# Issuing the four stores of the rotary tables from GpSimd instead of ScalarE in a hybrid mixer and MoE layer

## The chip, the cores and the metric

One Trainium2 chip, one core. The metric is device time in microseconds (us) of one execution of the whole layer. TensorE is called PE in the profile, VectorE DVE, ScalarE ACT, GpSimd POOL, SyncE SP.

## What is computed

One layer of a conditioned decoder on 1024 tokens of width 1024: a modulated layer norm, one input projection `h @ w_in`, three branches that read it (a gated short convolution, a diagonal state space model called S5, and latent attention with rotary positions), their gated merge, and a mixture-of-experts feed-forward. The change touches the rotary tables and lies in time next to S5:

```python
inv_freq = ROPE_THETA ** (-jnp.arange(0, QK_ROPE, 2, dtype=jnp.float32) / QK_ROPE)
ang = positions.astype(jnp.float32)[..., None] * inv_freq
return jnp.cos(ang), jnp.sin(ang)
...
mag = jnp.exp(ar * dt)
lb_re = mag * jnp.cos(ai * dt)
lb_im = mag * jnp.sin(ai * dt)
...
_, _, s_re, s_im = lax.associative_scan(combine, (la_re, la_im, bu_re, bu_im), axis=1)
```

## The kernel before, in words

The order of every engine's instructions is set when the program is built. In the stretch `front` the orders of DVE, ACT and PE are written out by hand; elsewhere a scheduler places each instruction by times that it simulates, and it may slip instructions of other parts into the hand-written stretch. Each engine then works strictly in that order and waits where an operand is missing.

`front` normalises x, transposes it in eight column blocks j (PE, tile `ps_x`, L570), scales and shifts each block (ACT, `ht`, L579, then its rounded half `hh`, L583; DVE makes the rest `hl`, L587) and at once multiplies it with three column tiles of `w_in`, the S5 inputs u (PE, L596).

`s5_params` works on POOL alone: exponentials and one sine and cosine (`sincos`) of 144 columns, 16 for the S5 poles and 128 for the rotary angles. The results are `sn`, `cs` and the negated sine `nsn`. Four transfers (L791) write them to the DRAM tensor `csd`; it is read back much later, by L882 for the keys and by L1171 for the attention. From the first 16 columns POOL goes on to the pole powers `lam`, `bbar` and `z8`.

`s5_prep` runs for the four quarters q of S5. POOL computes the matrices `X` (L752 to L757 with 128x512 operands), the phase table `T` (the same lines, doubling from 4 columns) and clears a buffer `Y` (L990). PE transposes `X` (L968), ACT copies the result to `W` (L970), a small kernel matrix `kq` goes through eight ACT transfers into `Y` (L992), and DVE reorders it into `M` (L993). `s5_run` multiplies u by `W` (PE, L1013), rotates by `T`, scans and rotates back on DVE (L1021 to L1029, then L752 to L757 into `s`), and multiplies by `M` and `G` (PE, L1041 and L1046); ACT copies the sums (L1051) and SP stores them.

Between these PE steps the scheduler sets independent work of PE: the fourth u tile and the attention gates (`proj`, three matmuls L140 to L142 per block, with the weight tile split into `whi` by ACT, L125, and `wlo` by DVE, L129), then the projections for the attention in `proj_qkv` (L893, then tiles `cq`). DVE also has products for the convolution there (L342, L348) and, after S5, the norms of `proj_qkv` (L921 to L930).

Of the kernel before, what the change touches and what calls it, by code (L numbers as in the profile page):

```python
# [80 lines left out]
class K:  # L81
# [677 lines left out]
    def s5_params(self):  # L759

        nc, a, P = self.nc, self.a, self.s5p
        v = nc.gpsimd
        f = lambda n, *s: P.tile([128, *s], F32, name=n)
# [24 lines left out]
        csd = self.csd = self.dram.tile([2, 32, S], F32, name="csd")  # L788
        for dst, src in ((csd[0, 0:16], cs[:, 16:]), (csd[0, 16:32], cs[:, 16:]), (csd[1, 0:16], nsn[:]),
                         (csd[1, 16:32], sn[:, 16:])):  # L790
            nc.scalar.dma_start(out=dst.rearrange("f (b t) -> (f b) t", b=8), in_=src)  # L791

        self.lam = L = f("lam", 2, 9, 16)
        tmp = t_("ltmp", 4, 16)
# [17 lines left out]
        for i in range(9):  # L812
            src, dst = max(0, i - 3), max(0, i - 2)
# [1243 lines left out]
```

## Time and profile before

| quantity | us |
|---|---|
| time, median of 3 runs (1546.9 to 1547.45) | 1546.98 |
| the profiled execution, its own time | 1544.51 |
| its span, first to last instruction | 1542.8 |
| PE busy | 1391.5 |
| DVE busy | 950.7 |
| ACT busy | 478.9 |
| POOL busy | 373.7 |

The span is cut into views of windows, waits and timelines below; their times count from the start of the span, so 1.7 us of the profiled execution lie around it. The stretch that matters is 50 to 302 us.

### The profile page before, as it was taken

What the parts mean: (1) busy time and instruction counts of PE and PEld (TensorE: products, weight loads), DVE (VectorE), ACT (ScalarE), POOL (GpSimd) and SP (SyncE); (2) the same over time, 40 slices, a digit from 0 to 9 for tenths busy, and PEclk for the clock granted to TensorE, in tenths of its full rate; (3) what the DMA queues carried; (4) which work ended last, traced back from release to release, by engine and by line L of the source; (5) the groups of instructions that cost most, each with busy time, mean ns of one, the idle gap of its engine ahead of it and who ended that gap; (6) DMA issues with size and microseconds to landing.
All of it is one profiled execution on the core that took longest, in us unless ns stands there. A gap on an engine that the chain in (4) does not pass through costs nothing.

```text
span 1542.8 us, 19462 instructions
## 1 busy us (share of the span) xinstructions
PE 1391.5 (90%) x6866; PEld 990.3 (64%) x6866; DVE 950.7 (62%) x1652; ACT 478.9 (31%) x851; POOL 373.7 (24%) x571
## 2 busy tenths in 40 slices
PE   5589799479999999999799997999988999999966
PEld 3467678368888887787588886778887333333312
DVE  7464677899685555767477787868887111122128
ACT  6232112242223334222277774343611111111113
POOL 7999930000000000003501142510032111111110
PEclk9899999799999999999889999999999999999988
DMA  9232221132222237986500005654645798878726
GB/s 376 95 119 85 74 57 37 41 112 66 82 82 110 109 132 253 346 268 170 114 1 15 15 15 164 229 178 166 245 150 204 269 339 339 300 263 306 241 110 248
DMA packets 78056, 251.63 MB, mean 163 GB/s; under 512 B 15945, under 2 KB 27265, under 8 KB 68738
## 3 DMA queue, kind: packets, MB, share of 16 engines
q1 hardware_dynamic: 54096, 203.61, 38.4%
q10 hardware_dynamic: 15506, 25.73, 4.8%
q0 software_dynamic: 8352, 20.98, 4.2%
q8 instruction: 57, 0.93, 0.3%
q14 instruction: 45, 0.37, 0.1%
HBM read 302.53 MB, written 50.38 MB: 229 GB/s over the span
## 4 chain that ended last, share of the span: by engine, by line
PE 48%; issue 14%; DVE 13%; DMA 11%; POOL 10%; ACT 3%; ACTq 1%; SPq 0%; POOLq 0%; DVEq 0%
PE ps_mm L140 9%; PE ps_mm L141 9%; PE ps_mm L142 9%; DMA yd<-y,idx 7%; PE ps_up L140 3%; PE ps_up L141 3%; PE ps_up L142 3%; PE ps_O L1272 2%; PE ps_T L1258 2%; PE ps_S L140 1%; PE ps_S L142 1%; PE ps_S L141 1%; PE ps_y L1728 1%; POOL xg L1602 1%; POOL yd L1661 1%
## 5 line engine op out<-in xcount | busy, mean ns | idle before, releaser
L140 PE MATMUL ps_mm<-hh,wlo 128*128 128x512 f32 x304 | 123.4, 406 | 23.1 <-ACT sg L1075 15.5
L1138 POOL TENSOR_TENSOR mg<-mg,sg 128x512 f32<-128x512 f32 x16 | 23.4, 1474 | 496.0 <-DVE sg L1137 492.4
L1631 PE MATMUL ps_h<-wo,xt 128*64 128x512 f32 x480 | 130.9, 596 | 0.0
L142 PE MATMUL ps_mm<-hh,whi 128*128 128x512 f32 x304 | 122.8, 404 | 0.0
L141 PE MATMUL ps_mm<-hl,whi 128*128 128x512 f32 x304 | 122.4, 403 | 0.0
L1624 ACT COPY xt<-ps_tr 128x512 f32<-128x512 f32 x48 | 28.1, 585 | 245.9 <-PE ps_tr L1622 245.9
L1684 DVE TENSOR_TENSOR hd<-ps_h,hd 128x256 f32<-128x256 f32 x24 | 10.2, 425 | 126.9 <-ACT hd L1683 126.9
L1631 PE MATMUL ps_y<-wo,ht 128*64 128x512 f32 x288 | 87.6, 598 | 0.0
L125 ACT CAST whi<-raw 128x1024 fp32r<-128x1024 f32 (+1 forms) x45 | 46.8, 1040 | 129.9 <-PE ps_up L142 59.0
L1631 PE MATMUL ps_h<-ql,xt 128*64 128x512 f32 x192 | 87.0, 596 | 0.0
L140 PEld LDWEIGHTS ps_mm<-hh,wlo 128*128 128x128 f32 x304 | 58.7, 193 | 38.1 <-ACT sg L1075 16.1
L129 DVE TENSOR_TENSOR wlo<-raw,whi 128x1024 fp32r<-128x1024 f32 x44 | 61.1, 1388 | 26.6 <-ACT whi L125 26.6
L1631 PEld LDWEIGHTS ps_h<-wo,xt 128*64 128x64 f32 x480 | 38.6, 137 | 49.6 <-issue 49.6
L142 PEld LDWEIGHTS ps_mm<-hh,whi 128*128 128x128 f32 x304 | 58.6, 193 | 15.0 <-issue 1.1
L141 PEld LDWEIGHTS ps_mm<-hl,whi 128*128 128x128 f32 x304 | 58.8, 193 | 13.6 <-issue 0.2
L1602 POOL DMA_INDIRECT xg<-h2d,idx x26 | 26.4, 1015 | 166.5 <-PE ps_tr L1622 164.4
L1659 DVE SCALAR_TENSOR_TENSOR y<-ps_y,roww,g 128x512 f32<-128x512 f32 x48 | 36.0, 751 | 38.8 <-PE ps_y L1631 38.8
L1244 DVE TENSOR_REDUCE sm<-ps_S 128x1 f32<-128x256 f32 (+3 forms) x64 | 49.2, 770 | 10.7 <-PE ps_S L1241 10.3
L140 PE MATMUL ps_up<-ah,wlo 128*128 128x512 f32 x128 | 50.6, 403 | 5.2 <-ACT ah L125 2.9
L129 DVE TENSOR_TENSOR pl<-ps_T,ph 128x512 fp32r<-128x512 f32 (+1 forms) x80 | 45.9, 580 | 13.8 <-ACT ph L125 12.5
L140 PE MATMUL ps_mm<-wo,ml 128*128 128x512 f32 x128 | 50.0, 398 | 2.8 <-DVE sg L1354 2.8
L1648 DVE COPY ht<-ps_th 128x256 f32<-128x256 f32 x24 | 10.2, 424 | 67.5 <-PE ps_th L1646 67.5
(674 smaller groups left out, 3938.8 us busy)
## 6 DMA issues: line engine op xcount, KB each, us to landing
wo<-exp SPq DMA_DIRECT2D x110, 1024.0 KB
qh<-exp SPq DMA_DIRECT2D x26, 1024.0 KB
ql<-exp SPq DMA_DIRECT2D x26, 1024.0 KB
raw<-w_in SPq DMA_DIRECT2D x43, 512.0 KB
adr<-w_ada SPq DMA_DIRECT2D x32, 512.0 KB
wada<-w_ada SPq DMA_DIRECT2D x16, 512.0 KB
fy<-yd SPq DMA_DIRECT2D x16, 512.0 KB
sga<-sg ACTq DMA_DIRECT2D x8, 512.0 KB
```

What stands on the lines that cost most here:

```text
L125: nc.scalar.copy(out=hi, in_=src)
L129: e.tensor_tensor(out=lo, in0=src, in1=hi.bitcast(F32), op=ALU.subtract)
L140: mm(ps, wl, xh, start=first, stop=False)
L141: mm(ps, wh, xl, start=False, stop=False)
L142: mm(ps, wh, xh, start=False, stop=last)
L1244: v.tensor_reduce(out=sm[:], in_=x, axis=AX.XY if two else AX.X, op=ALU.max, negate=True)
L1258: pe.transpose(pt[:, k2 * 256 + qi * 128:k2 * 256 + qi * 128 + 128], prob[h, c, qi][:, ks], self.ident[:])
L1272: pe.matmul(po[:, 0:256], vv[:, kt, h].rearrange("p z d -> p (z d)"), x[z], start=kt == 0 and z == 0, stop=kt == 2 * c + 1 and z == 1)
L1602: self.nc.gpsimd.indirect_dma_start(out=self.xg[b % 2][:], out_offset=None, in_=self.h2d[:], in_offset=bass.IndirectOffsetOnAxis(ap=self.i ...
L1624: self.nc.scalar.copy(out=self.ex[b][:, n * 512:(n + 1) * 512], in_=ps[:])
L1631: self.nc.tensor.matmul(ps[z * 64:(z + 1) * 64, :], x[:, z * 64:(z + 1) * 64], w[z], start=first, stop=last, tile_position=(0, 64 * z))
L1659: nc.vector.scalar_tensor_tensor(out=y[:, sl], in0=ps[:], scalar=self.roww[:, b:b + 1], in1=self.g2[:, sl], op0=ALU.mult, op1=ALU.mult)
```

## The change

The loop that issues the four transfers calls GpSimd's queue instead of ScalarE's. Data, sizes and destinations stay the same.

```diff
         for dst, src in ((csd[0, 0:16], cs[:, 16:]), (csd[0, 16:32], cs[:, 16:]), (csd[1, 0:16], nsn[:]),
                          (csd[1, 16:32], sn[:, 16:])):
-            nc.scalar.dma_start(out=dst.rearrange("f (b t) -> (f b) t", b=8), in_=src)
+            nc.gpsimd.dma_start(out=dst.rearrange("f (b t) -> (f b) t", b=8), in_=src)
```

On ACT the four transfers stood between the pieces of `front`: two ahead of the two `ht` of block 6 and two behind them; they are gone there. On POOL they now stand in the middle of `s5_params`, at the end of `sincos`:

```order
 L787 TENSOR_SCALAR nsn<-sn 128x128
+L791 DMA csd<-sn 128x128
 L798 TENSOR_TENSOR lam<-mag,sn 128x16
 L811 COPY z_757<-sn 128x16
 L748 TENSOR_TENSOR cs_662<-c,p 128x144
+L791 DMA csd<-nsn 128x128
 L753 TENSOR_TENSOR ltmp<-lam 128x16
 L827 TENSOR_TENSOR t_626<-lam,par 128x16
 L829 TENSOR_TENSOR f_806<-lam,par 128x16
 L816 TENSOR_TENSOR z_757<-z_757 128x16
+L791 DMA csd<-cs_662 128x128 x2
```

Everything else of POOL moved only by a few places among its own rows.

Because the scheduler simulates other times, the other engines' orders shift. On PE, 60 gate and projection matmuls of 512 columns stand ahead of the first L968 instead of 44; the difference is 15 to 28 through most of S5 and closes by its end: 368 stand ahead of the last quarter's L1046 in both.

On DVE, in the third quarter's `s5_run` (`w`, `xw`, `s` are its tiles, `wlo` belongs to a projection on PE, `raw` to the convolution products):

```order
 L755 TENSOR_TENSOR s<-w,T 128x4x127
 L1029 SCALAR_TENSOR_TENSOR w<-m_753,w 128x128 x4
+L993 COPY M<-Y 128x8x8x16
+L129 TENSOR_TENSOR wlo<-raw,whi 128x1024
 L753 TENSOR_TENSOR xw<-w,T 128x4x127
-L993 COPY M<-Y 128x8x8x16
-L129 TENSOR_TENSOR wlo<-raw,whi 128x1024
+L342 TENSOR_TENSOR raw<-hh_187,hl_193 128x1024
 L754 TENSOR_TENSOR s<-s,xw 128x4x127
-L342 TENSOR_TENSOR raw<-hh_187,hl_193 128x1024
 L756 TENSOR_TENSOR xw<-w,T 128x4x127
 L757 TENSOR_TENSOR s<-s,xw 128x4x127
```

The copy L993 of the last quarter's `M` now stands ahead of one more step (L753) of the third quarter.

On DVE again, a little later, in the last quarter's `s5_run`, before the change:

```order
L1026 TENSOR_TENSOR w<-w,xw 128x512
L1029 SCALAR_TENSOR_TENSOR w<-m_753,w 128x128 x4
L753 TENSOR_TENSOR xw<-w,T 128x4x127
L752 TENSOR_TENSOR s<-w,T 128x4x127
L755 TENSOR_TENSOR s<-w,T 128x4x127
L754 TENSOR_TENSOR s<-s,xw 128x4x127
L756 TENSOR_TENSOR xw<-w,T 128x4x127
L757 TENSOR_TENSOR s<-s,xw 128x4x127
L129 TENSOR_TENSOR wlo<-raw,whi 128x1024
L348 TENSOR_TENSOR raw<-raw 128x512
L907 COPY cq<-ps_mm 128x512 x2
L897 TENSOR_TENSOR nt_2018<-ps_mm,nt_2018 64x512
```

and with the change, the same place:

```order
L1026 TENSOR_TENSOR w<-w,xw 128x512
L129 TENSOR_TENSOR wlo<-raw,whi 128x1024
L1029 SCALAR_TENSOR_TENSOR w<-m_753,w 128x128 x4
L348 TENSOR_TENSOR raw<-raw 128x512
L753 TENSOR_TENSOR xw<-w,T 128x4x127
L752 TENSOR_TENSOR s<-w,T 128x4x127
L755 TENSOR_TENSOR s<-w,T 128x4x127
L754 TENSOR_TENSOR s<-s,xw 128x4x127
L756 TENSOR_TENSOR xw<-w,T 128x4x127
L757 TENSOR_TENSOR s<-s,xw 128x4x127
L907 COPY cq<-ps_mm 128x512 x2
L897 TENSOR_TENSOR nt_2018<-ps_mm,nt_2018 64x512
```

One `wlo` and one L348 moved from behind the last quarter's final `s` to a place ahead of it. From L907 on the orders agree.

## Rows read from the trace of the kernel before

**Rows 1.** Waits, 0 to 300 us: total us, times, longest us

```profile
ACT ht L579 <- DMA csd<-sn: 24.4, 1, 24.4
PE ps_x L570 <- ACT ht L579: 19.1, 2, 18.2
```

**Rows 2.** Timeline of ACT and PE at the stall: start us, us, [idle before <- releaser]

```profile
50.21 1.05 ACT L583 CAST hh<-ht 128x1024 fp32r<-128x1024 f32 x1
...
75.71 0.78 ACT L579 ACTIVATE ht<-ps_x,col 128x512 f32<-128x512 f32 x1 [24.45 <-DMA csd<-sn]
...
76.54 1.12 PE L570 MATMUL ps_x<-ident,x 128*128 128x128 f32 x4 [18.17 <-ACT ht L579]
...
78.16 2.06 PE L596 MATMUL ps_mm<-hh,wlo 128*128 128x512 f32 x4
...
84.77 1.10 PE L596 MATMUL ps_mm<-hl,whi 128*128 128x512 f32 x4
...
89.89 0.62 PE L596 MATMUL ps_ua<-hl,whi 128*128 128x512 f32 x2
```

**Rows 3.** Waits of POOL, 50 to 240 us, the whole answer

```profile
POOL s L1033 <- PE ps_ss L1046: 19.2, 1, 19.2
```

**Rows 4.** Windows: stretch, length, busy of each engine (x), PEclk, DMA, GB/s

```profile
core 0: us, PE busy (x) PEld busy (x) DVE busy (x) ACT busy (x) POOL busy (x), PEclk, DMA share, GB/s
57.50:74.00 16.50, 0.87 (x4) 0.38 (x2) 0.00 (x0) 0.00 (x0) 15.61 (x44) 0.67 0.00 0
...
185.00:208.80 23.80, 21.87 (x141) 16.66 (x140) 12.58 (x16) 5.64 (x11) 21.74 (x48) 0.86 0.43 119
208.80:240.00 31.20, 30.99 (x204) 24.23 (x203) 24.72 (x45) 4.24 (x6) 0.11 (x1) 1.00 0.21 35
240.00:302.00 62.00, 44.28 (x189) 35.10 (x187) 57.15 (x73) 11.75 (x17) 0.00 (x0) 0.89 0.06 14
```

**Rows 5.** Timeline of PE, its waits inside S5

```profile
103.65 0.66 PE L968 MATMUL ps_ss<-ident,X 128*128 128x128 f32 x4 [1.73 <-POOL X L754]
...
179.51 1.11 PE L968 MATMUL ps_ss<-ident,X 128*128 128x128 f32 x4 [6.18 <-POOL X L757]
...
231.90 0.49 PE L1046 MATMUL ps_ss<-s,G 64*128 64x128 f32 x4 [0.21 <-DVE s L757]
```

**Rows 6.** POOL's transfers: L1140 by tile (ns min/median/max), in the timeline, L1602

```profile
L1140 POOL DMA_DIRECT2D mgd<-mg x8: 553/566/798, 722.1 to 753.0; - x8
...
736.85 0.55 POOL L1140 DMA_DIRECT2D mgd<-mg  x1 [0.30 <-POOL mg L1138]
...
L1602 POOL DMA_INDIRECT xg<-h2d,idx x26 | 26.4, 1015 | 166.5 <-PE ps_tr L1622 164.4
```

**Rows 7.** Timeline: the end of POOL's work and what follows it

```profile
207.82 0.95 POOL L990 MEMSET Y<- 128x1024 f32 x1
...
208.80 5.27 ACTq L992 DMA_DIRECT2D Y<-kq  x8
...
216.63 0.69 DVE L993 COPY M<-Y 128x1024 f32<-128x1024 f32 x1 [1.17 <-DMA Y<-kq]
...
231.16 0.69 DVE L757 TENSOR_TENSOR s<-s,xw 128x508 f32<-128x508 f32 x1
```

**Rows 8.** Timeline of DVE: the three instructions that change sides there

```profile
214.77 0.69 DVE L753 TENSOR_TENSOR xw<-w,T 128x508 f32<-128x508 f32 x1
...
232.39 1.23 DVE L129 TENSOR_TENSOR wlo<-raw,whi 128x1024 fp32r<-128x1024 f32 x1 [0.54 <-ACT whi L125]
233.65 0.69 DVE L348 TENSOR_TENSOR raw<-raw 128x512 f32<-128x512 f32 x1
```

**Rows 9.** Timeline of DVE and POOL at one moment

```profile
78.98 1.22 DVE L587 TENSOR_TENSOR hl<-ht,hh 128x1024 fp32r<-128x1024 f32 x1 [22.53 <-ACT hh L583]
...
78.69 0.22 POOL L756 TENSOR_TENSOR ltmp<-lam 128x16 f32<-128x16 f32 x1
...
79.07 1.22 POOL L828 TENSOR_TENSOR f<-f,t 128x16 f32<-128x16 f32 x1
```

**Rows 10.** Timeline of DVE and PE behind S5

```profile
240.62 1.28 DVE L897 TENSOR_TENSOR nt<-ps_mm,nt 64x512 f32<-64x512 f32 x2 [5.08 <-ACT nt L896]
...
304.49 0.79 PE L140 MATMUL ps_mm<-hh,wlo 128*128 128x512 f32 x1 [15.54 <-ACT sg L1075]
```

## Prediction

> **What bounds the kernel now.** I read the table of waits of the first 300 us first, because the transfers lie there. It has one large entry with the changed line in it: ACT stands 24.4 us before a `ht` of `front`, released by the transfer `csd<-sn`, and PE stands 18.2 us behind ACT [rows 1]. The timeline shows how: ACT's last `hh` starts at 50.21, then ACT's queue holds the store of `sn`, whose data POOL has only at 74, and the `ht` behind it starts at 75.71; PE resumes at 76.54 and ends the u projection at 89.89 + 0.62 = 90.5 [rows 2]. This wait the change removes.
>
> Next I asked what sets the time after it. The waits of POOL from 50 to 240 us are one line, a wait of 19.2 us before the last small memset, after its work is done [rows 3]; until 208.8 POOL never waits for another engine. PE does wait for POOL: 1.73 us at the first transposition of `X`, 6.18 us at the fourth quarter's [rows 5]. And the last quarter ends on POOL's chain: the memset of `Y` ends at 208.77, ACT's eight transfers start at 208.80, DVE has stood 1.17 us when it copies `M` at 216.63, its rotations run without a gap to 231.85, and PE has stood 0.21 us when it takes `s` at 231.90 [rows 5, 7]. So in this stretch POOL paces S5, and the early stall of PE costs nothing that PE does not lose again when it waits for `X`. After S5, DVE is busy 57.15 of 62 us until 302 and PE waits 15.54 us for that chain [rows 4, 10]; a shift of the end of S5 goes through.
>
> **The change, part by part.** Removed: the 18.17 us of PE. With them gone the u projection ends near 90.5 - 18 - 2 = 70.5; the 2 are the first 4 us or so after the idle, in which four matmuls took 2.06 us against 1.10 later, the granted clock having fallen to 0.67 in the idle stretch [rows 2, 4]. What comes next on PE is a fourth u tile and twelve gate matmuls, 60 in all, at 1.10/4 = 0.27 us or less, so PE stands before the first `X` by 70.5 + 16 = 87. POOL finishes that `X` just before 103.65 [rows 5] plus its own delay. PE waits at least 16 us there: the stall moves, it does not go. The order gives PE a lead of 16 matmuls, some 4 us, that closes by the last quarter (368 ahead of it in both). Gain booked: 0, hidden by POOL.
>
> Added on POOL: four issues. Before they cost POOL nothing. The nearest rows are its own plain stores of 128 rows: 0.55 to 0.80 us, median 0.566, the next instruction starting only behind it, and 0.30 us more where the transfer waits for the POOL instruction just ahead [rows 6]. Two of the four have such a wait in the built order. I take 4 x 0.566 + 2 x 0.30 = 2.9 us. Bounds: 4 x 0.55 = 2.2 without those waits, 4 x 1.015 + 0.6 = 4.7 at the price of its gathers [rows 6]; the plain store is the nearer relative. Nothing hides it, since POOL has no slack until 208.8.
>
> The page "SBUF — State Buffer" of the Trainium skill, section "SBUF: two separate sides", speaks against the change: a transfer issued from GpSimd can stand still because VectorE locks GpSimd out of a shared port while it writes descriptors, and it says to issue from ScalarE or SyncE instead. Rows show such a lock in another form: while a DVE subtraction of 1.22 us ran, a POOL product that is as small as its 0.22 us neighbour took 1.22 us, 1.0 more [rows 9]. At that price each of the four issues would cost 1.0 more, 4 us; I book none, because DVE has little to do when they are issued (it waits for `lam`, which POOL computes behind them).
>
> The same collision in the other direction: four DVE instructions (two `hl`, two `wlo`) that met POOL's small products after 78 now meet `sincos` between 58 and 75, where DVE had been idle [rows 4, 9]. Each costs POOL about 1.0 us there and gives it back later; I book 0, with plus or minus 2 as bounds.
>
> Moved on DVE: `M` of the last quarter comes when POOL's memset, ACT's transfers and their landing allow, at 216.63 plus the 2.9. DVE gets there early in either order (before: 1.17 us early). But three instructions that stood outside the path from this copy to the last `s` now stand inside it: L753 (0.69, was ahead of the copy), `wlo` (1.23) and L348 (0.69), both formerly behind the last `s` [rows 8]. Sum 2.6 us. The lower bound is 0, if DVE comes to the copy so early or late that the order does not bind. Those behind S5 are no gain: DVE stood 5.08 us before L897 anyway [rows 10].
>
> Sum: 2.9 + 2.6 = 5.5 us later at the end of S5, near 237.4 instead of 231.9. PE arrives there some 7 us before that and idles; DVE's chain to 302 has under 5 us of gaps, most of them waits of its own chain, so the 5.5 stay. The rest of the program has the same order and comes 5.5 later: span 1548.3, and 1550.0 for an execution like the profiled one. The median of the runs lies 2.5 above that execution, so 1546.98 + 5.5 = **1552.5 us**.
>
> **The rivals.** (1) POOL is not the pace, PE is, and the removed stall comes through: 18 us less, minus the 2.9 of the issues, about 1532. For it: the wait of 24.4 us is the longest single one of the first 300 us [rows 1]. Against it: POOL without a wait until 208.8, and PE waiting for `X`. It decides from the point at which POOL reaches its last memset more than 5.5 us sooner than I think. In a small form, POOL gaining 6 to 9 us because DVE's work collides less with it, it gives 1540 to 1543.
>
> (2) Only part of the 5.5 shows: the DVE order does not bind, 2.9 left, 1549.9; or the collisions give 2 back and 3.5 stay, 1550.5; or both and nothing is left. That is within 0.2% (3.1 us, about what this kernel's timing can tell from no change) or just at it.
>
> (3) The lock reaches the issues: 4 us more, 1556.5. The skill's rule above would give this. The same size would come from PE's clock: a 7 us idle ahead of the last L1046 could leave PE at the lower level for some matmuls behind it, each group of four costing 1 us more [rows 2], 2 us in all.
>
> **How the numbers follow.** The forecast (3.1 to 8 us slower) 0.50; rival 2 (within 3.1 us) 0.25; rival 1 in both forms 0.15; rival 3 (over 8 us slower) 0.10. Slower by over 0.2% is 0.50 + 0.10 = 0.60, same 0.25, faster 0.15. The range leaves out the large form of rival 1 and the tail of rival 3: 1543.5 (3.5 faster) to 1557.5 (10.5 slower).
>
> **What would show it.** Right: no ACT wait for `csd` in the new trace; PE idle 15 to 22 us before the first L968; POOL busy without waits until about 211.7 with four L791 issues near 75 to 80, each 0.55 to 0.8 us; the last `s` near 237; PE's L140 that stood at 304.49 near 310. Wrong: if POOL's last memset ends before 208 the POOL term fails; if it ends at 211 to 212 but the last `s` at 234 or 235 the DVE term fails; if PE does not stand before L968, POOL was not the pace.

## The result, and the profile after

The change makes the kernel slower. In the first comparison the median is 1555.78 us after against 1546.94 before (ratio 1.0056, 95% interval 1.0042 to 1.0070), and in a second one 1553.29 against 1547.41 (1.0049, 1.0032 to 1.0066). That is 7.6 to 8.7 us more by the ratios. The profiled execution took 1555.84 us with a span of 1554.1, 11.3 more than the span of before.

The stall is gone from ACT and from PE. Here is the window that stood empty in [rows 4], and PE's timeline at its first wait for `X` and at the L140 behind S5:

```profile
core 0: us, PE busy (x) PEld busy (x) DVE busy (x) ACT busy (x) POOL busy (x), PEclk, DMA share, GB/s
57.50:74.00 16.50, 16.14 (x75) 12.87 (x74) 4.96 (x4) 8.37 (x12) 15.61 (x33) 1.00 0.26 88
```

```profile
103.85 1.11 PE L968 MATMUL ps_ss<-ident,X 128*128 128x128 f32 x4 [19.02 <-POOL X L754]
...
314.60 0.79 PE L140 MATMUL ps_mm<-hh,wlo 128*128 128x512 f32 x1 [15.22 <-ACT sg L1075]
```

PE works 16.14 of the 16.5 us in which it had 0.87, and then stands 19.02 us, where it had stood 1.73, in front of an `X` that comes at 103.85 instead of 103.65 [rows 5]. The stall moved. The L140 that started at 304.49 [rows 10] starts at 314.60.

The next rows follow the path through S5 from a POOL row of `sincos` that comes ahead of all rows that the change moves on POOL and DVE. They are rows of POOL's timeline; its only wait from 50 to 240 us is the 20.17 us of the last one, after its work is done:

```profile
57.89 0.42 POOL L713 TENSOR_TENSOR z<-r 128x144 f32<-128x144 f32 x1
...
78.79 0.82 POOL L791 DMA_DIRECT2D csd<-sn  x1
...
80.39 0.61 POOL L791 DMA_DIRECT2D csd<-nsn  x1
...
81.72 1.12 POOL L791 DMA_DIRECT2D csd<-cs  x2
...
212.49 0.95 POOL L990 MEMSET Y<- 128x1024 f32 x1
...
233.60 0.11 POOL L1033 MEMSET s<- 128x8 f32 x1 [20.17 <-DVE raw L348]
```

then of DVE and of ACT:

```profile
220.03 0.69 DVE L993 COPY M<-Y 128x1024 f32<-128x1024 f32 x1 [5.66 <-DMA Y<-kq]
...
221.78 0.68 DVE L753 TENSOR_TENSOR xw<-w,T 128x508 f32<-128x508 f32 x1
...
223.51 0.68 DVE L754 TENSOR_TENSOR s<-s,xw 128x508 f32<-128x508 f32 x1
...
230.53 1.22 DVE L129 TENSOR_TENSOR wlo<-raw,whi 128x1024 fp32r<-128x1024 f32 x1
...
232.95 0.66 DVE L348 TENSOR_TENSOR raw<-raw 128x512 f32<-128x512 f32 x1
...
236.76 0.69 DVE L757 TENSOR_TENSOR s<-s,xw 128x508 f32<-128x508 f32 x1
...
249.64 1.28 DVE L897 TENSOR_TENSOR nt<-ps_mm,nt 64x512 f32<-64x512 f32 x2 [11.00 <-ACT nt L896]
```

```profile
245.29 1.07 ACT L1051 COPY Y<-ps_ss 128x512 f32<-128x512 f32 x2 [10.68 <-PE ps_ss L1046]
```

Before, the POOL row L713 started at 58.05, DVE's L754 of the third quarter at 218.37 and ACT's last L1051 at 236.33:

```profile
58.05 0.42 POOL L713 TENSOR_TENSOR z<-r 128x144 f32<-128x144 f32 x1
...
218.37 0.68 DVE L754 TENSOR_TENSOR s<-s,xw 128x508 f32<-128x508 f32 x1
...
236.33 1.07 ACT L1051 COPY Y<-ps_ss 128x512 f32<-128x512 f32 x2 [3.97 <-PE ps_ss L1046]
```

So the path from L713 to L1051 is 178.28 us before and 187.40 after, 9.12 longer. Its four pieces, with the other ends from [rows 7]: POOL from L713 to the end of the last `Y` 150.72 and 155.55 (+4.83); from there to `M` 7.86 and 6.59 (-1.27); from `M` to the end of the last `s` 15.22 and 17.42 (+2.20); from that `s` to L1051 4.48 and 7.84 (+3.36). The last piece is PE's, and the forecast did not have it in its sum. PE's timeline shows why it grew; first before, then after:

```profile
232.32 0.71 PE L1041 MATMUL ps_ss<-U,M 128*128 128x128 f32 x4
232.97 0.71 PE L1046 MATMUL ps_ss<-s,G 64*128 64x128 f32 x8
```

```profile
224.34 0.80 PE L1046 MATMUL ps_ss<-s,G 64*128 64x128 f32 x4 [4.35 <-DVE s L754]
...
236.15 0.80 PE L1046 MATMUL ps_ss<-s,G 64*128 64x128 f32 x4 [1.49 <-DVE s L754]
237.50 0.80 PE L1046 MATMUL ps_ss<-s,G 64*128 64x128 f32 x4 [0.55 <-DVE s L757]
238.23 1.22 PE L1041 MATMUL ps_ss<-U,M 128*128 128x128 f32 x4
```

Windows of PE after (stretch, length, PE busy and its rows, PEclk, DMA share, GB/s):

```profile
215.00:220.00 5.00, 4.99 (x22) 1.00 0.24 57
220.00:225.00 5.00, 0.67 (x4) 0.87 0.00 0
225.00:230.00 5.00, 5.00 (x25) 0.50 0.01 3
...
240.00:245.00 5.00, 5.00 (x30) 0.50 0.01 1
245.00:250.00 5.00, 5.00 (x19) 0.74 0.52 75
```

In an idle of 4.35 us the granted clock falls from 1.00 to 0.50, the lower of its two levels (1.2 instead of 2.4 GHz), and it is back only in the window from 245 to 250. The same group of four L1041 takes 1.22 us instead of 0.71. Before, PE had not idled there and the clock was 1.00 [rows 4]. What PE waits for in this idle is the third quarter's L754 on DVE, which starts 5.14 us later than before: `M`, ahead of it in both orders, comes 3.40 us later, and from `M` to L754 it takes 3.48 us instead of 1.74, because L753 and L342 now stand between the two. So the new order on DVE, besides lengthening the piece from `M` to `s`, has a part in PE's idle.

The other 2.3 us of the 11.3 lie behind L1051 (1308.81 against 1306.47 us), where the order is the same. In the kernels below with one of these two orders that remainder runs from 1306.6 to 1313.2 us, so I put it down to scatter.

### The profile page after: what moved, and what is told of

Same layout as the page of the kernel before. It is cut to its first block, busy times and chain, and to the rows that moved or that the text cites. A ratio compares the mean times of both kernels' runs of the same rounds, so it can differ in the third digit from the quotient of the medians.

```text
span 1554.1 us, 19469 instructions
## 1 busy us (share of the span) xinstructions
PE 1398.3 (90%) x6866; PEld 996.4 (64%) x6866; DVE 955.2 (61%) x1652; ACT 479.3 (31%) x851; POOL 381.1 (25%) x575
## 5 line engine op out<-in xcount | busy, mean ns | idle before, releaser
L140 PE MATMUL ps_mm<-hh,wlo 128*128 128x512 f32 x304 | 125.0, 411 | 22.7 <-ACT sg L1075 15.2
L1684 DVE TENSOR_TENSOR hd<-ps_h,hd 128x256 f32<-128x256 f32 x24 | 10.2, 425 | 126.9 <-ACT hd L1683 126.9
L140 PEld LDWEIGHTS ps_mm<-hh,wlo 128*128 128x128 f32 x304 | 59.5, 196 | 39.3 <-ACT sg L1075 15.9
L1602 POOL DMA_INDIRECT xg<-h2d,idx x26 | 26.4, 1016 | 166.0 <-PE ps_tr L1622 163.3
L1244 DVE TENSOR_REDUCE sm<-ps_S 128x1 f32<-128x256 f32 (+3 forms) x64 | 49.2, 770 | 10.8 <-PE ps_S L1241 10.0
L140 PE MATMUL ps_up<-ah,wlo 128*128 128x512 f32 x128 | 50.6, 403 | 5.1 <-ACT ah L125 2.9
L1258 PE MATMUL ps_T<-ident,p 128*128 128x128 f32 x288 | 48.8, 278 | 4.9 <-DVE p L1248 2.3
L140 PE MATMUL ps_mm<-wo,ml 128*128 128x512 f32 x128 | 49.6, 395 | 3.7 <-DVE sg L1354 2.8
```

Of the source, the lines that this page charges most:

```text
L140: mm(ps, wl, xh, start=first, stop=False)
L1244: v.tensor_reduce(out=sm[:], in_=x, axis=AX.XY if two else AX.X, op=ALU.max, negate=True)
L1258: pe.transpose(pt[:, k2 * 256 + qi * 128:k2 * 256 + qi * 128 + 128], prob[h, c, qi][:, ks], self.ident[:])
L1602: self.nc.gpsimd.indirect_dma_start(out=self.xg[b % 2][:], out_offset=None, in_=self.h2d[:], in_offset=bass.IndirectOffsetOnAxis(ap=self.i ...
```

## The experiments

The scheduler had answered the change with other orders on PE, DVE, ACT and POOL, so the change mixes two things: who issues, and in which order all else stands. Most kernels below fix the order: a table holds the order of the rows of `before` or of the change, by instruction name, and an edge between neighbours on one engine sets the issue order without adding a wait.

```diff
+def keep_order(self):
+    info = mybir.DependencyInfo(mybir.DependencyClass.NoSync, mybir.DependencyReason.DATA)
+    by = {i.name: i for i in self.nc.cur_bb.bb.instructions}
+    for text in ORDER.values():
...
+        for p, q in zip(row, row[1:]):
+            self.tc.add_manual_dep(by[q], p, info, reason="order")
```

The table gives for each kernel the four pieces of the path in one profiled execution, read as above, their sum, and the median of its runs with the ratio to the kernel before, which ran with it.

| kernel | L713 to end of `Y` | to `M` | to end of `s` | to L1051 | sum | median | ratio, 95% interval |
|---|---|---|---|---|---|---|---|
| before | 150.72 | 7.86 | 15.22 | 4.48 | 178.28 | 1546.94 | |
| order_before_sp | 150.50 | 7.52 | 15.23 | 4.48 | 177.73 | 1548.19 | 1.0000 (0.9984, 1.0016) |
| order_before_pool | 154.00 | 7.18 | 15.23 | 7.55 | 183.96 | 1551.54 | 1.0025 (1.0007, 1.0043) |
| order_after_act | 151.84 | 6.96 | 17.42 | 7.85 | 184.07 | 1552.98 | 1.0038 (1.0022, 1.0053) |
| order_after_sp | 151.65 | 6.75 | 17.42 | 6.35 | 182.17 | 1551.08 | 1.0018 (1.0003, 1.0033) |
| after | 155.55 | 6.59 | 17.42 | 7.84 | 187.40 | 1555.78 | 1.0056 (1.0042, 1.0070) |
| after_again | 153.98 | 6.59 | 17.42 | 7.84 | 185.83 | 1553.29 | 1.0049 (1.0032, 1.0066) |
| after_filled | 153.74 | 6.59 | 17.43 | 7.85 | 185.61 | 1555.07 | 1.0044 (1.0024, 1.0064) |
| after_filled_twice | 154.07 | 6.62 | 17.42 | 6.01 | 184.12 | 1552.91 | 1.0034 (1.0019, 1.0049) |
| after_dve_order | 154.44 | 6.59 | 13.08 | 7.84 | 181.95 | 1547.94 | 1.0003 (0.9987, 1.0018) |
| after_sp_dve_order | 151.41 | 6.76 | 13.08 | 7.85 | 179.10 | 1548.57 | 1.0013 (1.0001, 1.0025) |
| after_sp_dve_order_filled | 151.63 | 6.75 | 13.08 | 7.58 | 179.04 | 1547.33 | 1.0000 (0.9986, 1.0014) |
| z8_on_dve_act | 143.26 | 6.95 | 17.95 | 8.42 | 176.58 | 1551.31 | 1.0033 (1.0016, 1.0051) |
| z8_on_dve_sp | 141.28 | 7.57 | 17.98 | 7.78 | 174.61 | 1549.60 | 1.0016 (1.0001, 1.0031) |

Single runs of one kernel scatter by more than 10 us (the kernel before, in one comparison: 1540.4 to 1553.18), so a time decides about 2 to 3 us at best, and smaller questions are read from the path. The path scatters too: after and after_again, which have the same rows, differ by 1.57 us.

**Who issues, in either order.** The first kernel moves the stores to SP; the scheduler then gives the order of `before` on PE, DVE and POOL by itself. The other three fix the order.

```diff
-            nc.gpsimd.dma_start(out=dst.rearrange("f (b t) -> (f b) t", b=8), in_=src)
+            nc.sync.dma_start(out=dst.rearrange("f (b t) -> (f b) t", b=8), in_=src)
```

> The four csd stores are issued by SP; every engine's row order is that of the kernel before, less the four stores on ACT. Theory (POOL paces the S5 stage, so the removed stall only moves): ACT's and PE's stall at 57 to 75 us is gone, PE idles 15 to 20 us before the first L968 instead, the first L968 stays within 0.5 us of 103.65, and the time is that of the kernel before within 2 us: 1545 to 1549. Rival (PE's work is the pace): the 14 us that PE gets back come through, 1532 to 1535. Second rival (SP's queue is held by the waiting store and the U and w_kr loads behind it come late): over 1550.

PE's timeline at the first wait for `X`:

```profile
101.64 1.11 PE L968 MATMUL ps_ss<-ident,X 128*128 128x128 f32 x4 [20.34 <-POOL X L754]
```

The stall is gone and PE stands 20.34 us before the first `X` instead. The path is 0.55 us shorter, the ratio 1.0000; its interval leaves room for 2.5 us either way. The rival in which PE is the pace (1532 to 1535) is out, and the median is also under that of the second rival (over 1550). L968 came 2 us earlier than expected; 1.6 of it is L713, which started at 56.45 here.

For order_before_pool the change keeps its stores on POOL and gets the table of `before`:

```diff
-            stream.close()
+            stream.close(); self.keep_order()
```

> POOL issues the four stores, as in the change, but every other row on every engine stands where it stood in the kernel before. Theory (the POOL issues cost about 2.9 us, the new order of DVE and PE costs the rest): 1549 to 1551, that is 2 to 4 over the kernel before; the last memset of Y ends 2.5 to 3.5 us later than 208.8 and PE keeps its full clock from 225 to 245 us. Rival (the issues and what they lock cost it all, the order nothing): 1554 to 1557, like the change.

POOL's rows with the order of `before`, without the stores and with them:

```profile
75.77 0.53 POOL L787 TENSOR_SCALAR nsn<-sn 128x128 f32<-128x128 f32 x1
...
77.74 0.22 POOL L797 TENSOR_TENSOR lam<-mag,cs 128x16 f32<-128x16 f32 x1
```

```profile
77.20 0.54 POOL L787 TENSOR_SCALAR nsn<-sn 128x128 f32<-128x128 f32 x1
...
77.69 0.82 POOL L791 DMA_DIRECT2D csd<-sn  x1
...
81.76 0.24 POOL L797 TENSOR_TENSOR lam<-mag,cs 128x16 f32<-128x16 f32 x1
```

From L787 to L797 it takes 1.97 us without the stores and 4.56 with them: the four issues cost POOL 2.59 us, and nothing hides them. To the end of `Y` it is 3.50 us (154.00 against 150.50); the 0.9 more is within the scatter of this piece, which runs from 153.74 to 155.55 in the five profiles of the change's order on PE and POOL with the stores on POOL. The time is 0.5 us over the bracket, and one expectation was wrong: PE's clock did not hold. In the order of `before`, too, POOL's lateness alone makes PE idle longer ahead of the last group (1.22 and 0.86 us, against 0.54 and 0.86 with the stores on SP), the granted clock from 235 to 240 us is 0.50, and the piece behind `s` goes from 4.48 to 7.55. So 3.50 us on POOL become 6.23 on the path.

For order_after_sp and order_after_act the table of the change is used, with the stores on SP and on ACT (the edit above with the other engine).

> Every engine's row order is that of the change, but the four stores are issued by SP, so POOL carries none. Theory (the order costs 5 to 6 us by itself: three DVE instructions ahead of the last s, and PE's idle of 4.4 us after which its clock is at 0.5 until 247 us): 1552 to 1554; PE's granted clock from 225 to 245 us is about 0.5 again. Rival (the order costs nothing, all of it was POOL's issues): 1546 to 1548.

> Every engine's row order is that of the change, but the four stores are issued by ACT at their old place, so ACT's and PE's stall at 58 to 75 us is back. Theory (the removed stall is worth nothing, the order costs 5 to 6 us): 1552 to 1555, the same as with SP within 1.5 us. Rival (the stall's removal is worth several us and the change hides it): 4 or more us above the kernel with SP, 1557 and up.

The order alone, with no store on POOL, lengthens the path by 3.9 us (182.17 against 178.28), less than the 5 to 6 expected; the median of 1551.08 lies 1 us under the bracket of the theory and 3 over that of the rival. The `M` to `s` piece is 17.42 in every kernel with this order and 15.2 in every kernel with the other. With ACT's stall put back the time is 1.9 us higher, a little over the 1.5 expected. Of the path's 1.9 us, 1.5 lie behind `s`, where the granted clock from 235 to 240 us is 0.50 with ACT and already 0.81 with SP, while the end of `Y` differs by 0.2. The rival of a hidden gain (4 and more) is not seen in the medians or the path; the ratios alone, 0.0020 apart with about 0.0015 either way each, would not exclude it. Taken together, the ratios say 0.25% for the stores on POOL in the old order, 0.18% for the new order without them, and 0.49 to 0.56% for both: each of the two costs something by itself, and both together come near the sum of 0.43%.

**The DVE order alone.** PE, ACT, POOL and SP as in the change; four rows of DVE behind the last `s`, and L753 ahead of `M`:

```diff
+L753 TENSOR_TENSOR xw<-w,T 128x4x127
 L993 COPY M<-Y 128x8x8x16
-L129 TENSOR_TENSOR wlo<-raw,whi 128x1024
-L753 TENSOR_TENSOR xw<-w,T 128x4x127
-L342 TENSOR_TENSOR raw<-hh,hl 128x1024
...
-L129 TENSOR_TENSOR wlo<-raw,whi 128x1024
...
-L348 TENSOR_TENSOR raw<-raw 128x512
...
 L757 TENSOR_TENSOR s<-s,xw 128x4x127
+L129 TENSOR_TENSOR wlo<-raw,whi 128x1024
+L342 TENSOR_TENSOR raw<-hh,hl 128x1024
+L129 TENSOR_TENSOR wlo<-raw,whi 128x1024
+L348 TENSOR_TENSOR raw<-raw 128x512
```

> The change, row for row on PE, ACT, POOL and SP; on DVE the two wlo (L129), L342 and L348 that stand between the last M (L993) and the last s (L757) stand behind that s, and L753 ahead of M: 4.6 us of DVE work out of that stretch. Theory (the stretch is DVE-bound and on the path): from M to the end of s 12.8 us instead of 17.4, the time 1550 to 1552. Rival (DVE has slack there, or PE then waits for wlo as long): within 1 us of 1555.8.

DVE's timeline:

```profile
217.52 0.69 DVE L993 COPY M<-Y 128x1024 f32<-128x1024 f32 x1 [3.74 <-DMA Y<-kq]
...
229.91 0.69 DVE L757 TENSOR_TENSOR s<-s,xw 128x508 f32<-128x508 f32 x1
230.52 1.22 DVE L129 TENSOR_TENSOR wlo<-raw,whi 128x1024 fp32r<-128x1024 f32 x1
```

From `M` to the end of `s` it is 13.08 us, 4.34 less, and the time is back at that of the kernel before (1.0003), 2 us under the expected bracket. DVE's order in this stretch is on the path. The time fell by more than the piece (5 to 8 us by the medians), which the scatter of the runs allows and the path does not explain: it is still 3.67 us longer than before.

**PE's clock.** Matmuls with zero weights, which add nothing to a bank that is open, fill the idle:

```diff
-        mm(ps, wh, xl, start=False, stop=False)
+        mm(ps, wh, xl, start=False, stop=False); [mm(ps, self.zw[:], xh, start=False, stop=False) for _ in range(zeros)]
```

> The change, row for row, with 18 more matmuls of 128x512 with zero weights that add nothing to the bank that the projection ahead has open, placed in PE's idle of 4.35 us ahead of the L1046 at 224.3, and one DVE instruction at the start that makes the zeros. Theory (PE's clock, which falls to 0.5 after that idle, costs 3.4 us between the last s and the copy L1051): the clock from 225 to 245 us stays at 1.0, the stretch from the last s to L1051 goes from 7.85 to about 4.5 us and the time to 1552 to 1553. Rival (the low clock costs nothing on the path): within 1 us of 1555.8.

A miss: the time is within 1 us of the change, as the rival said. The clock held at the first place, but PE, now faster, came earlier to the last group, stood 4.47 us there, and lost the clock then; the piece is 7.85 as in the change. So this run does not decide whether the clock costs time, and a second filling went to the last group, in `s5_run`:

```diff
-                                 M[:, gi].rearrange("p j d -> p (j d)"), U[:, gi, :], start=True, stop=False)
+                                 M[:, gi].rearrange("p j d -> p (j d)"), U[:, gi, :], start=True, stop=False); [nc.tensor.matmul(py[0][:, 0:128], self.zf[:], U[:, gi, :], start=False, stop=False) for _ in range(N2 if (q, gi) == (3, 1) else 0)]
```

> The change, row for row, with both of PE's idle times ahead of its last two groups of L1046 filled by matmuls with zero weights that add nothing (18 of 128x512 ahead of the L1046 at 224.3, 14 of 128x128 ahead of the last group, where the kernel with one filling idled 4.47 us and lost the clock). Theory (the low clock costs 3.3 us on the path): the granted clock is 1.0 in all of 220 to 245 us, the stretch from the last s to L1051 is 4.5 to 4.9 us instead of 7.85, and the time 3 to 4 us under the change. Rival (the low clock does not reach the end): within 1 us of the change.

Its windows of PE:

```profile
230.00:235.00 5.00, 3.63 (x35) 1.00 0.60 90
235.00:240.00 5.00, 4.14 (x26) 0.66 0.09 15
240.00:245.00 5.00, 5.00 (x34) 1.00 0.17 23
```

Half succeeded. Two idle times of 1.36 and 0.86 us remained, the clock was low for part of one window, and the piece went to 6.01: 1.83 of the 3.36 us came back. The time is 0.4 us under that of after_again, inside the scatter. The rows show that the clock sets this piece; that it carries through to the end the times do not settle.

> The change itself, on the same chip as the three kernels below, for comparison with them. It should stand 7 to 10 us above the kernel before, 1554 to 1557. If it stands only 5 to 6 above, the forecast's size was right and the first figure was scatter.

It stands 5.9 us above by the medians, under the expected 7 to 10, and 7.6 by the ratio, inside it. With its interval of 5.0 to 10.2 us it does not exclude the forecast's 5.5. The first comparison (6.5 to 10.8) does, but on four runs of each kernel, and a profile of the change is 1.57 us apart from another of the same rows; how far the forecast was short is known to some 3 us either way.

**Together.** SP issues, the order of the change with DVE's four rows moved; then also 12 zero matmuls ahead of the last group.

> The order of the change, the stores issued by SP, and on DVE the four instructions moved behind the last s. Theory (the terms add up): POOL's issues 3.9 and DVE's order 4.3 us come off the 187.4 us between the L713 at 57.89 and L1051, to 178 or 179, as long as the kernel before: the time within 1.5 us of the kernel before, 1545.5 to 1548.5. Rival (the two overlap): 3 or more us above the kernel before.

> The same, with 12 matmuls of 128x128 with zero weights in PE's idle of some 4 us ahead of the last group of L1046, so that the clock stays. Theory: 3.3 us below the kernel above, 1542 to 1545, which beats both kernels. Rival (the clock falls in another idle time instead, or PE is not on the path there): no faster than the kernel above.

The path comes to 179.10, as the terms add up to, and the time to 1.0013 (1.0001 to 1.0025), just outside the bracket at its upper end. The filling did not hold the clock here (7.58), so the last kernel is no test of it; it missed the expected 1542 to 1545 and is as fast as the kernel before and no faster. No version here beats the kernel before.

**POOL relieved.** The small products for `z8` go to DVE, behind its last `hl`, with the stores on ACT and on SP; between the two only the stores differ.

```diff
-        z = f("z8", 8, 2, 16)
+        z = f("z8", 8, 2, 16); after = self.tc.issue_after(self.last_low.ins); after.__enter__()
...
-            v.tensor_tensor(out=z[:, 7, 0], in0=s0, in1=s0, op=ALU.mult)
+            nc.vector.tensor_tensor(out=z[:, 7, 0], in0=s0, in1=s0, op=ALU.mult)
...
```

> The kernel before, with the powers of z8 (47 small instructions, 16.4 us of POOL's busy time in the kernel with the stores on SP) computed by DVE behind its last hl, so POOL's chain is shorter; ACT still issues the csd stores and stalls. Theory (POOL paces S5): the last memset of Y comes 8 to 14 us earlier than 208.8 and the time falls to 1534 to 1541, short of the full 16 us because PE and DVE, which lost 16 us to the stall, become the pace. Rival (POOL does not pace S5): 1545 to 1549, POOL waits instead.

> The same with the csd stores issued by SP, so that the stall on ACT and PE at 58 to 75 us is gone as well; every other row stands as in the kernel with the stores on ACT and z8 on DVE. Theory (the removed stall is worth nothing only as long as POOL is the pace): now it is worth something, the time is 2 to 8 us below that kernel, 1530 to 1537. Rival (the stall's removal is worth nothing whatever POOL does): within 1.5 us of that kernel.

Both were misses in time: 4.7 and 3.0 us above the kernel before by the medians, where 5 us and more below it were expected. POOL's piece shrinks by 7.5 and 9.2 us, but the scheduler's new order takes it back: 18 us from `M` to `s`, 7.8 to 8.4 behind it, and 68.6 us from L897 to the first activation L1075 behind S5, which take 63.2 in the kernel before. So these two do not show what a shorter POOL chain is worth; that POOL's delay reaches the end of S5 is shown by order_before_pool. What the expectations left out is that a shorter POOL chain gets another order everywhere. Without the stall the path is 2.0 us shorter and the median 1.7 lower, between the 2 to 8 expected and the rival's 1.5; the intervals overlap. Nor is PE free of a stall in the second kernel. It stands for `wlo`, which DVE now makes behind the powers of `z8`, for which DVE in turn waits 12.10 us until POOL has `cs`:

```profile
83.56 0.79 PE L140 MATMUL ps_mm<-hh,wlo 128*128 128x512 f32 x1 [13.18 <-DVE wlo L129]
```

Whether the stall's removal is worth something with POOL relieved stays open.

## Why the prediction was right, and where it was off

**The stall moves and gives nothing.** Right, and shown to within 2.5 us: with the order unchanged and the stores on SP the stall is gone, PE stands 20.34 us before `X`, and the ratio is 1.0000 (0.9984 to 1.0016).

**POOL's four issues, 2.9 us.** Right: 2.55 us of issue rows, 2.59 of delay in the same order. In all profiles with the order of the change, POOL's piece averages 154.36 us with the stores on POOL (five profiles) and 151.56 with them on SP (three), a difference of 2.8. The lock of rival 3 did not come: DVE ran nothing from 72.49 to 93.78 us, and the issues stood at 78.79 to 82.84, as the prediction had argued. DVE's next row in the change:

```profile
93.78 1.23 DVE L752 TENSOR_TENSOR G<-lam,cc 128x512 f32<-128x512 f32 x1 [21.30 <-POOL lam L754]
```

The price here is the time that the issues themselves take (0.82 and 0.61 us, and two in 1.12) on an engine without slack. The Trainium skill (page "SBUF — State Buffer", section "SBUF: two separate sides") advises to issue from ScalarE or SyncE, because VectorE can lock GpSimd out while it writes descriptors. The advice agrees with these runs, in which POOL was the wrong queue; its reason was not tested by any of them, since no DVE row ran beside the issues.

**POOL against DVE, booked at 0 with plus or minus 2.** Within the bounds. The order of the change lengthens POOL's piece by about 1 us with no store in it (151.56 against 150.50), three profiles against one, so within the scatter. The first profile of the change has 1.2 more than the mean of its kind; single POOL rows of the same order differ between two profiles by 0.5 to 1.0 us in either direction (a row L755 of `T` took 1.20 us there and 0.22 in after_again).

**From `Y` to `M`, taken as unchanged.** It became 1.27 us shorter, in all kernels with the order of the change by 0.9 to 1.3. The eight issues of L992 take 0.2 of it (5.06 us after, 5.27 before); the other 1.06 lie between the end of the last issue and `M` (1.50 us after, 2.56 before), that is, in the landing of the last transfer. Why it lands sooner stays open.

**DVE's order, 2.6 us.** Right: 17.42 against 15.22 us, 2.20. The durations of [rows 8] sum to 2.6, but neighbours on DVE start before the one ahead has ended (L753 at 221.78 and the row behind it at 222.38), so each adds less than it lasts: 0.60, 1.13 and 0.58 us.

**The place of the last `s`, 237.4.** It ends at 237.45, but in part by luck: POOL's piece grew by 4.83 us instead of 2.9, `Y` to `M` shrank by 1.27 that nobody booked, DVE's order gave 2.20 instead of 2.6, and L713 started 0.16 earlier.

**The term that was wrong:** "PE arrives there some 7 us before that and idles". I booked this idle as free and gave the clock 2 us and a place in rival 3, as two groups of four matmuls at 1 us more each; that is not "the same size" as the 4 us of the lock beside it, as the prediction has it. PE came 2.8 us ahead of the last `s`, not 7. It idled 4.35 us one quarter earlier, ahead of the third quarter's L1046, the clock stayed low until the last group, and there seven groups, from L1046 at 237.50 on, took 0.3 to 0.5 us more each: 3.36 us on the path. With 2.8 for POOL's issues, about 1 for the order on POOL, -1.3, 2.2 and 3.4 the sum of the path is 8.1 us, against 7.6 and 8.7 by the two ratios. That the 3.4 reach the end of the program is not shown by the times: holding half of it changed the median by 0.4 us. So the mechanism of the forecast was the one that happened, and the likely reason why its size was short is the clock.

## What to carry to other kernels

A stall whose waiting engine soon waits again, for an engine without slack, was worth nothing here; what it is worth once that engine is relieved, no run here shows. Moving work onto that engine to remove the stall costs its full time (2.59 us for four issues). A delay of some us ahead of a burst of matmuls can nearly double (3.50 us on POOL, 6.23 on the path in order_before_pool), because the idle that it leaves lowers PE's clock for the burst; so ask of each idle what PE does right behind it. Where a scheduler answers an edit with another order, fix the order and change one thing at a time before giving the edit the blame.

## What was not expected of the hardware

The same POOL row in the same place of the same order takes different times in two executions. In order_before_sp and then in order_before_pool, whose rows agree up to there:

```profile
32.01 0.31 POOL L731 TENSOR_SCALAR h<-h 128x144 f32<-128x144 f32 x1
32.29 0.21 POOL L690 TENSOR_TENSOR r<-r,p 128x16 f32<-128x16 f32 x1
```

```profile
32.70 1.37 POOL L731 TENSOR_SCALAR h<-h 128x144 f32<-128x144 f32 x1
34.04 1.18 POOL L690 TENSOR_TENSOR r<-r,p 128x16 f32<-128x16 f32 x1
```

About 1 us each, the size of the collision in [rows 9], and DVE's rows fit it. In order_before_sp both POOL rows are over before DVE's `wlo` starts; in order_before_pool, where POOL comes 0.7 us later, they run beside it and the row behind it:

```profile
32.62 1.25 DVE L651 TENSOR_TENSOR wlo<-raw,whi 128x1024 fp32r<-128x1024 f32 x1 [2.46 <-ACT whi L648]
```

```profile
32.67 1.23 DVE L651 TENSOR_TENSOR wlo<-raw,whi 128x1024 fp32r<-128x1024 f32 x1 [2.46 <-ACT whi L648]
33.81 1.32 DVE L559 SCALAR_TENSOR_TENSOR wada<-wada,crow 128x1024 f32<-128x1024 f32 x1
```

L713 starts at 56.4 to 56.7 us in some profiles and at 57.8 to 58.1 in the others. Such a difference travels to the end of S5: in order_before_sp L713 starts 1.60 us and L1051 2.15 us earlier than in the kernel before, whose rows have the same order. It is why the path is counted from L713.
